# A hybrid decoder layer: expert gathers one block further ahead, other leads of the streams, adaLN loads by GpSimd, and a closing norm in groups of two

## The chip, the cores and the metric

The kernel runs on 1 core of one Trainium2 chip. The metric is the device time of one execution in microseconds (us), the median of several runs. Engines are named as in the profile: PE (TensorE matmul), PEld (TensorE weight load), DVE (VectorE), ACT (ScalarE), POOL (GpSimd) and SP (SyncE, which only issues transfers here).

## The reference

One decoder layer on 1024 tokens of width 1024, all in float32. `mod = silu(c) @ ada_w + ada_b` gives six rows of 1024 (shift, scale and gate for each half of the layer). The first half is a token mixer: FoX attention on 8 heads and an RWKV-7 recurrence on 8 heads, both from one input projection. The second half is a mixture of experts: 64 experts, 6 chosen per token, plus a shared one. The layer closes with an RMS norm.

```python
mod = jax.nn.silu(c) @ ada_w[l] + ada_b[l]
sh1, sc1, g1, sh2, sc2, g2 = jnp.split(mod[:, None, :], 6, axis=-1)
h = rms_norm(x, norm1_g[l]) * (1 + sc1) + sh1
z = h @ w_in[l]
...
x = x + g1 * (jnp.concatenate([y_fox, y_rwkv], axis=-1) @ w_out[l])
h = rms_norm(x, norm2_g[l]) * (1 + sc2) + sh2
x = x + g2 * moe_ffn(h, ...)    # sum over a token's experts of w_e * (silu(h Wg) * (h Wu)) Wd, plus the shared expert
return rms_norm(x, final_g)
```

## The kernel before, in words

**Order of the work.** Every engine executes its own queue in the order in which the program emits the instructions, and the kernel writes that order itself. `phase_a` holds some forty generators ("streams", one for each kind of work). `weave` (L1296) is a planner: it keeps a model clock for each engine, and always advances the stream whose next step is the earliest, after its lead has been taken off (L1361); a stream with a larger lead is emitted earlier than its place by the model clock. The leads are the numbers in the list at L1283 to L1292. They move instructions within each engine's queue, DMA issues among them; they add or remove none. `warm` (L169) puts dummy matmuls where the planner expects PE to be idle.

**Streams that the change touches.** `tok` (L756) turns RWKV features into token order by PE, copies them out by ACT and stores them. `main` (L670) forms these features, `gates` (L560) their gate, `merge` (L802) joins the halves of a triangular inverse, and `a4["gate"]` (L1484) gates the mixers' outputs ahead of the output projection. `adaln` (L1241) calls `mods_gen` (L1371): four rows of `mod`, each from eight tiles of 128x1024 weights (`mw`, 512 KB, three buffers) that SP loads (L1380); even tiles are multiplied and summed by DVE, odd ones scaled by ACT (L1393) and added by DVE. This runs beside the RWKV chain of 16 steps (`chain`, L918) and the attention.

**The expert blocks.** `experts` (L2091) runs 92 blocks: 8 of the shared expert (in token order), then 84 of the routed ones in a fixed order, each up to 128 rows. A routed block needs its slots (`need_s`, L2050: POOL gathers the token numbers and weights, tile `sl`, 8 buffers), its rows (`need_x`, L2060: POOL gathers rows of `d_h2` into `xg`, 4 buffers), and at its end `result` (L2022): DVE writes `ye` (3 buffers) and POOL adds it to `d_acc` in memory by an indirect DMA with `compute_op=add`. Every such addition goes to the same tensor, so it waits for the one before it to have landed. `need_t` (L2056) only makes a view of `sl`; it issues nothing. In iteration b, PE computes the gate and up products of block b (`up`), turns block b-1's activation (`act_t`), turns the rows of block b+1 (`turn`, tile `tp`), and computes block b-1's down product (`down`, tile `yd`). When an expert is new, DVE and ACT split its raw weights (`gate`, `up`, `down`) into two halves (L1897, L1898, L1904, L1905), and SP fetches weights three experts ahead. For b > 7, POOL's queue in iteration b holds, in this order:

```python
need_x(b + 3)                                             # L2124: gather rows, 3 blocks ahead
need_s(b + 5)                                             # L2126: gather slots, 5 blocks ahead
result(zs, blocks[b - 1][2], weight_of(b - 1), tis[b - 1])  # L2156: add block b-1 to d_acc
```

`dispatch` (L2077) gathers the slots of blocks 8 to 12 ahead of the loop. `rest` (L2170) handles overflow blocks, none in this input's profile.

**The closing norm.** `final` (L2198) loads eight tiles of 128x1024 from `d_acc`, squares them by ACT, forms the inverse root of a group of four by POOL (`rstd_pow`, L142), multiplies by DVE and stores.

Of the kernel before, what the change touches and what calls it, by code (L numbers as in the profile page):

```python
# [8 lines left out]
F32 = mybir.dt.float32  # L9
# [11 lines left out]
D = 1024  # L21
# [16 lines left out]
class Kern:  # L38
# [296 lines left out]
    def phase_a(self, psum):  # L335
# [51 lines left out]
        def loader():  # L387
            for j in range(1, len(tiles)):
                yield [("wait", ("raw used", j - 1))]
                load(j)  # L390
                yield [("set", ("raw", j))]
# [884 lines left out]
        def swap_project():  # L1276
# [4 lines left out]
            yield [("set", ("block pools", 0))]  # L1281

        self.weave([(swap_rwkv(), 9), (swap_fox(), 9),  # L1283
                    (chain(), -1.2), (inverse(), 2), (merge(), 2), (zts(), -2.3), (prods(), 1.5), (feeds(), 10.3),
                    (mixes(), 15.2), (kappa(), 1.2), (pre(), 1), (main(), 1),
                    (tok(), 2.2), (setup(), 0), (gates(), -0.5), (loader(), 0), (weights(), 3.3),
                    (fgate(), 1.8), (fk(), 1.8), (fv(), 0.8), (fq(), -0.5), (proj(), 0.6),
                    (ld(), 1.9), (rowmax(), 0.1), (exps(), 0.3), (onorm(), 0), (ynorm(), 1.1), (adaln(), -2),
                    (swap_ff(), 2.2), (swap_chain(), 0), (a4["router"](), -0.5), (a4["routes"](), -0.5), (a4["post"](), -0.2),
                    (a4["weights"](), 2), (swap_fox_out(), 9.6), (swap_project(), 16.6),  # L1290
                    (b["shared"](), -2.7), (b["dispatch"](), -0.2), (b["experts"](), -3.5),
                    (a4["gate"](), 0.8), (a4["project"](), -0.3), (a4["loads"](), -1)])  # L1292
        b["rest"]()

    @staticmethod
# [75 lines left out]
    def mods_gen(self, wp, pp):  # L1371

        nc, A = self.nc, self.A
        for m in range(4):
# [2 lines left out]

            def load(k):
                w = wp.tile([128, D], F32, name="mw", bufs=3)
                nc.sync.dma_start(w, A["ada_w"][0, k * 128:(k + 1) * 128, c0:c0 + D])  # L1380
                return w
            ws = [load(0), load(1)]
            yield [("DMA", 3.0)]
# [459 lines left out]
    def phase_b(self, pg, close_a4, h2):  # L1843
# [84 lines left out]
            yield [("set", ("shared w", 0))]  # L1928

        def slots(idx, n):  # L1930
            sl = B["fp"].tile([128, 2], F32, name="sl", bufs=8)
            nc.gpsimd.indirect_dma_start(out=sl[0:n], out_offset=None, in_=self.d_slot, in_offset=ind(idx[0:n]))  # L1932
            return sl

# [142 lines left out]
        def dispatch():  # L2077
            yield [("wait", ("route", 7))]
            expert_pools()
            yield from self.ranks(pg)  # L2080
            for k in range(1, 4):
                need_w(k)
            yield from self.leftover(pg)
            yield [("wait", ("block pools", 0))]
            for b in range(8, 13):
                need_s(b)
                yield [("POOL", 1.0)]
            yield [("DMA", 4.0)]
            yield [("set", ("slots", 0))]

        def experts():  # L2091
# [13 lines left out]
            for b in range(NB + 1):  # L2105
                if b < NB:
                    k, j, n = blocks[b]
                    m = max(n, MIN_M)
                    two = xt[1] is None
                    for s in up(xt, sets[k % 2], m):  # L2110
                        if b < 8:
                            yield s
                    z = B["z"]
                    if b < 5:
                        yield [("wait", ("T", blocks[b + 3][1]))]
                        need_x(b + 3)
                    elif b == 6:
                        yield [("wait", ("slots", 0))]
                        for i in range(8, 12):
                            need_t(i)  # L2120
                        need_x(8)
                        need_x(9)
                    elif b > 6:
                        need_x(b + 3)  # L2124
                    if b > 7:
                        need_s(b + 5)  # L2126
                    turnover = k + 1 < NK + 1 and (blocks[b - 1][0] != k if k else b == 6)
                    if turnover and k + 1 < NK:
                        work.append(split_gu(raws[k + 1], k + 1))
                    pieces(3)  # L2130
                    if turnover and b < 8:
                        yield [("~ACT", 1.7), ("~DVE*", 1.8)]
# [26 lines left out]
                if b < NB:  # L2159
                    if k and blocks[b - 1][0] != k:  # L2160
                        work.append(split_d(rawd[k]))
                        pieces(99)
                    if b > 7:
                        need_t(b + 4)
                    if turnover:
                        need_w(k + 4)
                    if turnover and b < 8:
                        yield [("~ACT", 2.0), ("~DVE", 2.3), ("~POOL", 1.0)]
# [29 lines left out]
    def final(self):  # L2198
        tc, nc, A = self.tc, self.nc, self.A
        with self.pool(name="fin", bufs=1) as fp:  # L2200
# [6 lines left out]
                nc.sync.dma_start(x, self.d_acc[i * 128:(i + 1) * 128, :])  # L2207
                xs.append(x)
            sm = fp.tile([128, 3, 8], F32, name="sm")
            for g in range(0, 8, 4):  # L2210
                gs = slice(g, g + 4)
                for i in range(g, g + 4):
                    sq = fp.tile([128, D], F32, name="sq", bufs=2)
                    nc.scalar.activation(sq, xs[i], AF.Square, accum_out=sm[:, 0, i:i + 1])  # L2214
                for _ in self.rstd_pow(sm[:, 1, gs], sm[:, 0, gs], D, 1e-6):
                    pass
                for i in range(g, g + 4):
                    nc.vector.scalar_tensor_tensor(xs[i], xs[i], sm[:, 1, i:i + 1], fg, op0=OP.mult, op1=OP.mult)  # L2218
                    nc.sync.dma_start(self.out[0, i * 128:(i + 1) * 128, :], xs[i])

# [41 lines left out]
```

## Time and profile before

| | us |
|---|---|
| median of 3 runs | 2097.12 |
| lowest and highest run | 2080.12, 2115.2 |
| the profiled execution, its own time | 2093.02 |
| its span, first to last instruction | 2091.1 |
| PE busy | 1858.6 (89%) |
| DVE busy | 1470.3 (70%) |
| ACT busy | 933.1 (45%) |
| POOL busy | 859.6 (41%) |
| mean granted TensorE clock, share of full | 0.918 |

The profiled execution took 1.9 us beyond its span, and was 4.1 us shorter than the median of the runs. Busy times are averages over stages with different limits. The stages on the span, about: start 0 to 50, projection and RWKV features to 450, chain and attention to 1000, output projection and routing to 1200, expert blocks to 2060, closing norm to 2091.

### The profile page before, as it was taken

The page shows a single profiled execution, that of the slowest core. Times are in us where ns is not written, and L with a number is a line of the kernel's source. Part 1 is how long each engine was busy: PE and PEld are TensorE (multiplying, and loading weights), DVE is VectorE, ACT ScalarE, POOL GpSimd, SP SyncE. Part 2 cuts the span into 40 slices and gives each one's busy share as a digit, 9 for nine tenths or more (in the row PEclk, how much of TensorE's full clock was granted, in tenths as well). Part 3 has the DMA queues.
Part 4 walks back from the last instruction along what each step waited for, and adds up shares of the span by engine and source line. Part 5 has one row for each costly group of instructions (what it writes and reads, how often), then busy time and mean ns, then how long its engine had stood idle before and what let it go on. Part 6 is the DMA issues. An engine that isn't in the chain of part 4 may idle for free. (4 is left out here: it accounts for less than half of the span.)

```text
span 2091.1 us, 28436 instructions
## 1 busy us (share of the span) xinstructions
PE 1858.6 (89%) x9729; PEld 1399.2 (67%) x9729; DVE 1470.3 (70%) x2561; ACT 933.1 (45%) x1431; POOL 859.6 (41%) x660
## 2 busy tenths in 40 slices
PE   3999999969997997997999799989988989989993
PEld 3777677747876664654787687767756767766771
DVE  7736867939457555656677758878767878878894
ACT  5443433312322332344323236556545656666673
POOL 1201110100012232335455634765656767766662
PEclk7999789969987888998999899999989999999997
DMA  7125345462756648964664589989889999988874
GB/s 270 36 81 126 88 111 129 131 156 71 216 148 183 190 123 237 133 195 137 229 211 147 159 277 322 314 256 318 293 261 309 304 305 307 326 297 297 307 242 174
DMA packets 268579, 440.03 MB, mean 210 GB/s; under 512 B 127445, under 2 KB 197161, under 8 KB 242450
## 3 DMA queue, kind: packets, MB, share of 16 engines
q1 hardware_dynamic: 210978, 365.47, 54.0%
q0 software_dynamic: 26176, 58.91, 12.4%
q10 hardware_dynamic: 31280, 13.83, 2.5%
q8 instruction: 78, 1.28, 0.3%
q14 instruction: 67, 0.55, 0.1%
HBM read 355.27 MB, written 94.90 MB: 215 GB/s over the span
## 5 line engine op out<-in xcount | busy, mean ns | idle before, releaser
L2028 POOL DMA_INDIRECT d_acc<-ye,sl x84 | 192.1, 2287 | 253.4 <-issue 56.2
L1932 POOL DMA_INDIRECT sl<-d_slot,d_sidx x84 | 201.6, 2400 | 27.5 <-issue 24.7
L1904 ACT ACTIVATE wdh<-down 128x1024 fp32r<-128x1024 f32 x128 | 128.7, 1053 | 82.2 <-PE yd L1976 82.2
L1898 DVE TENSOR_TENSOR gul<-up,guh 128x1024 fp32r<-128x1024 f32 x128 | 155.5, 1215 | 10.4 <-ACT guh L1897 9.7
L1940 POOL DMA_INDIRECT xg<-d_h,sl x84 | 149.0, 1774 | 25.6 <-issue 20.7
L1898 DVE TENSOR_TENSOR gul<-gate,guh 128x1024 fp32r<-128x1024 f32 x128 | 155.2, 1213 | 1.7 <-ACT guh L1897 1.7
L1905 DVE TENSOR_TENSOR wdl<-down,wdh 128x1024 fp32r<-128x1024 f32 x128 | 150.1, 1210 | 0.8
L2026 DVE SCALAR_TENSOR_TENSOR ye<-yd,sl,g 128x512 f32<-128x512 f32 (+12 forms) x168 | 120.2, 740 | 32.0 <-PE yd L1976 32.0
L1897 ACT ACTIVATE guh<-gate 128x1024 fp32r<-128x1024 f32 x128 | 134.1, 1047 | 18.8 <-DMA gate<-in_exp_w_gate_dram 18.8
L1976 PE MATMUL yd<-wdh,ah 128*128 128x512 f32 (+6 forms) x368 | 130.5, 438 | 8.5 <-ACT ah L2012 6.7
L1897 ACT ACTIVATE guh<-up 128x1024 fp32r<-128x1024 f32 x128 | 135.1, 1055 | 1.5 <-DMA up<-in_exp_w_up_dram 1.5
L450 PE MATMUL zp<-hTh,whi 128*128 128x512 f32 x480 | 132.4, 414 | 1.4 <-ACT whi L373 1.4
L450 PE MATMUL zp<-hTl,whi 128*128 128x512 f32 x480 | 132.1, 412 | 0.0
L450 PE MATMUL zp<-hTh,wlo 128*128 128x512 f32 x480 | 131.9, 413 | 0.0
L1976 PE MATMUL gu<-guh,xh 128*128 128x512 f32 (+6 forms) x504 | 127.3, 394 | 0.8 <-ACT xh L1959 0.5
L1976 PE MATMUL gu<-guh,xl 128*128 128x512 f32 (+6 forms) x504 | 127.4, 395 | 0.1
L1976 PE MATMUL yd<-wdh,al 128*128 128x512 f32 (+6 forms) x368 | 123.4, 418 | 4.2 <-DVE al L2014 3.7
L1976 PE MATMUL gu<-gul,xh 128*128 128x512 f32 (+6 forms) x504 | 127.0, 394 | 0.0
L1976 PE MATMUL yd<-wdl,ah 128*128 128x512 f32 (+6 forms) x368 | 122.3, 415 | 0.3 <-DVE wdl L1905 0.3
L2012 ACT ACTIVATE ah<-g 128x256 fp32r<-128x256 f32 (+5 forms) x92 | 31.2, 339 | 179.0 <-PE g L2010 178.3
L450 PEld LDWEIGHTS zp<-hTh,whi 128*128 128x128 f32 x480 | 92.6, 198 | 26.4 <-issue 5.5
L1976 PEld LDWEIGHTS gu<-guh,xh 128*128 128x128 f32 (+6 forms) x504 | 89.1, 177 | 29.1 <-ACT xh L1959 1.0
(477 smaller groups left out, 4238.9 us busy)
## 6 DMA issues: line engine op xcount, KB each, us to landing
gate<-in_exp_w_gate_dram SPq DMA_DIRECT2D x64, 1024.0 KB
up<-in_exp_w_up_dram SPq DMA_DIRECT2D x64, 1024.0 KB
down<-in_exp_w_down_dram SPq DMA_DIRECT2D x64, 1024.0 KB
mw<-in_ada_w_dram SPq DMA_DIRECT2D x32, 512.0 KB
wraw<-in_w_in_dram SPq DMA_DIRECT2D x30, 512.0 KB
xw<-in_ada_w_dram SPq DMA_DIRECT2D x8, 1024.0 KB
xw<-in_x_dram SPq DMA_DIRECT2D x8, 512.0 KB
fb<-d_fb SPq DMA_DIRECT2D x16, 256.0 KB
```

Of the source, the lines that this page charges most:

```text
L450: nc.tensor.matmul(z, a[:, d, :], b[:, d, hs], start=(n == 0 and d == 0), stop=(n == 2 and d == 7))
L1897: nc.scalar.activation(gh[:, qs, n, :], t[:, qs], AF.Copy)
L1898: nc.vector.tensor_sub(gl[:, qs, n, :], t[:, qs], gh[:, qs, n, :].bitcast(F32))
L1904: nc.scalar.activation(dh[:, j], raw[0][:, j], AF.Copy)
L1905: nc.vector.tensor_sub(dl[:, j], raw[0][:, j], dh[:, j].bitcast(F32))
L1932: nc.gpsimd.indirect_dma_start(out=sl[0:n], out_offset=None, in_=self.d_slot, in_offset=ind(idx[0:n]))
L1940: nc.gpsimd.indirect_dma_start(out=x[0:n], out_offset=None, in_=self.d_h2, in_offset=ind(ti), bounds_check=T - 1, oob_is_err=False)
L1976: nc.tensor.matmul(z, x[:, d, :], w[:, d, cs], start=(m == 0), stop=(m == 3 * n - 1))
L2012: nc.scalar.activation(ah[:, :, 0:n], tp[:, :, 0:n], AF.Copy)
L2026: nc.vector.scalar_tensor_tensor(y[0:n, hs], zs[h][0:n], wt, B["g2"][0:n, hs], op0=OP.mult, op1=OP.mult)
L2028: nc.gpsimd.indirect_dma_start(out=self.d_acc, out_offset=ind(ti), in_=y[0:n], in_offset=None, bounds_check=T - 1, oob_is_err=False, compu ...
```

## The change

It does five things.

1. Rows of a block are gathered four blocks ahead (`need_x(b + 4)`), slots six ahead (`need_s(b + 6)`), with nine `sl` buffers for eight; `dispatch` gathers six blocks' slots ahead of the loop. POOL's order within an iteration stays: rows, slots, addition.
2. Five leads: `merge` 2 to 2.1, `main` 1 to 0.9, `tok` 2.2 to 1.4, `gates` -0.5 to -0.6, `a4["gate"]` 0.8 to 0.9.
3. The 32 loads of `mw` are issued by POOL, not SP.
4. `need_t` is called beside `need_s`; it issues nothing.
5. The closing norm works in groups of two tiles.

```diff
-                    (chain(), -1.2), (inverse(), 2), (merge(), 2), (zts(), -2.3), (prods(), 1.5), (feeds(), 10.3),
-                    (mixes(), 15.2), (kappa(), 1.2), (pre(), 1), (main(), 1),
-                    (tok(), 2.2), (setup(), 0), (gates(), -0.5), (loader(), 0), (weights(), 3.3),
+                    (chain(), -1.2), (inverse(), 2), (merge(), 2.1), (zts(), -2.3), (prods(), 1.5), (feeds(), 10.3),
+                    (mixes(), 15.2), (kappa(), 1.2), (pre(), 1), (main(), 0.9),
+                    (tok(), 1.4), (setup(), 0), (gates(), -0.6), (loader(), 0), (weights(), 3.3),
...
-                    (a4["gate"](), 0.8), (a4["project"](), -0.3), (a4["loads"](), -1)])
+                    (a4["gate"](), 0.9), (a4["project"](), -0.3), (a4["loads"](), -1)])
...
-                nc.sync.dma_start(w, A["ada_w"][0, k * 128:(k + 1) * 128, c0:c0 + D])
+                nc.gpsimd.dma_start(w, A["ada_w"][0, k * 128:(k + 1) * 128, c0:c0 + D])
...
-            sl = B["fp"].tile([128, 2], F32, name="sl", bufs=8)
+            sl = B["fp"].tile([128, 2], F32, name="sl", bufs=9)
...
-            for b in range(8, 13):
+            for b in range(8, 14):
                 need_s(b)
...
                     elif b == 6:
                         yield [("wait", ("slots", 0))]
-                        for i in range(8, 12):
+                        for i in range(8, 14):
                             need_t(i)
-                        need_x(8)
-                        need_x(9)
+                        for i in range(8, 10):
+                            need_x(i)
                     elif b > 6:
-                        need_x(b + 3)
+                        if b == 7:
+                            need_x(10)
+                        need_x(b + 4)
                     if b > 7:
-                        need_s(b + 5)
+                        need_s(b + 6)
+                        need_t(b + 6)
...
-                    if b > 7:
-                        need_t(b + 4)
...
-            for g in range(0, 8, 4):
-                gs = slice(g, g + 4)
-                for i in range(g, g + 4):
+            for g in range(0, 8, 2):
+                gs = slice(g, g + 2)
+                for i in range(g, g + 2):
...
-                for i in range(g, g + 4):
+                for i in range(g, g + 2):
                     nc.vector.scalar_tensor_tensor(xs[i], xs[i], sm[:, 1, i:i + 1], fg, op0=OP.mult, op1=OP.mult)
```

## Rows read from the trace of the kernel before

**Rows 1.** Windows: busy us (count) of PE PEld DVE ACT POOL, PEclk, DMA share, GB/s
```profile
400.00:1200.00 800.00, 708.16 (x4206) 525.25 (x4205) 499.75 (x1124) 243.01 (x415) 263.35 (x327) 0.90 0.62 168
1240.00:2040.00 800.00, 747.56 (x3463) 567.70 (x3462) 652.14 (x841) 487.81 (x712) 517.33 (x235) 0.96 0.90 294
```
**Rows 2.** Waits of PE, 1195 to 2060: total us, times, longest us
```profile
PE tp L1965 <- DMA xg<-d_h,sl: 39.1, 11, 9.8
PE tp L1952 <- DMA xg<-d_h,sl: 6.4, 2, 5.7
```
**Rows 3.** Timeline of PE around one stall, then the window behind it
```profile
1531.45 1.68 PE L1965 MATMUL tp<-idf,xg 108*128 108x108 f32 x8 [9.84 <-DMA xg<-d_h,sl]
...
1536.41 1.05 PE L1976 MATMUL yd<-wdh,ah 128*128 128x512 f32 x2
...
1546.62 0.62 PE L1976 MATMUL yd<-wdh,ah 128*72 128x512 f32 x2
...
1530.00:1540.00 10.00, 8.55 (x28) 6.46 (x29) 3.48 (x6) 4.28 (x6) 5.59 (x5) 0.59 0.47 88
```
**Rows 4.** Timeline of POOL, 1657 to 1698: start, us, what, [idle before]
```profile
1657.42 1.44 POOL L2028 DMA_INDIRECT d_acc<-ye,sl  x1 [0.30 <-issue]
1659.17 0.96 POOL L1940 DMA_INDIRECT xg<-d_h,sl  x1 [0.31 <-issue]
1660.43 6.32 POOL L1932 DMA_INDIRECT sl<-d_slot,d_sidx  x1 [0.30 <-issue]
1667.06 1.50 POOL L2028 DMA_INDIRECT d_acc<-ye,sl  x1 [0.30 <-DVE xl L1968]
...
1678.67 1.50 POOL L2028 DMA_INDIRECT d_acc<-ye,sl  x1 [2.00 <-DVE gul L1898]
...
1697.86 7.28 POOL L2028 DMA_INDIRECT d_acc<-ye,sl  x1 [4.45 <-DVE ye L2026]
```
**Rows 5.** Timeline of DVE: `ye` of the additions at 1678.67 and 1697.86
```profile
1668.76 1.40 DVE L2026 SCALAR_TENSOR_TENSOR ye<-yd,sl,g 96x512 f32<-96x512 f32 x2
...
1686.47 0.75 DVE L2026 SCALAR_TENSOR_TENSOR ye<-yd,sl,g 128x512 f32<-128x512 f32 x1 [0.65 <-PE yd L1976]
```
**Rows 6.** Instructions on `d_acc` and their landing, then POOL's sequencer at L2028
```profile
L2028 POOL DMA_INDIRECT d_acc<-ye,sl x84: 1362/1608/7284, 1236.7 to 2059.3; - x84
DMA to landing us min/median/max: 4.0/8.8/17.8
...
L2028 POOLq EVENT_SEMAPHORE  x83: 17/5240/17366, 1237.6 to 2058.5; - x83
```
**Rows 7.** adaLN loads: SP issues, waits of ACT and PE, one stall, POOL's own loads
```profile
L1380 SPq DMA_DIRECT2D mw<-in_ada_w_dram x32: 327/449/1693, 545.1 to 808.8; - x32
...
ACT mw L1393 <- DMA mw<-in_ada_w_dram: 40.2, 9, 10.5
...
PE pm L174 <- ACT yt L964: 11.1, 1, 11.1
...
786.20 2.17 SPq L1380 DMA_DIRECT2D mw<-in_ada_w_dram  x2
...
792.29 1.15 ACT L1393 ACTIVATE mw<-mw,sc 128x1024 f32<-128x1024 f32 x1 [10.48 <-DMA mw<-in_ada_w_dram]
...
L992 POOL DMA_DIRECT2D d_y<-yt x8: 597/620/670, 604.8 to 915.2; - x8
```
**Rows 8.** Waits of PE, 450 to 700: the longest stall of the feature streams
```profile
PE g L616 <- ACT sqk L1038: 15.3, 4, 13.5
```
**Rows 9.** The closing norm: end of the second square, POOL, DVE, memory rate
```profile
2071.98 0.19 ACT L2214 ACTIVATION_READ_ACCUMULATOR sq<-x 128x1 f32 x1
...
2075.16 1.04 POOL L146 TENSOR_TENSOR sm<-sm,blk 128x4 f32<-128x4 f32 x1
...
2076.24 4.87 DVE L2218 SCALAR_TENSOR_TENSOR x<-x,sm,fg 128x1024 f32<-128x1024 f32 x4 [17.31 <-POOL sm L146]
...
2070.00:2076.00 6.00, 0.00 (x0) 0.00 (x0) 0.00 (x0) 4.52 (x8) 1.03 (x2) 0.50 1.03 419
```

## The prediction

> **What bounds the kernel now.** I read the page's 40 slices first, then windows by stage, then who PE waits for in each stage, and at last the timelines of POOL, DVE and PE side by side. The reader is to see two stages that matter. From 400 to 1200 PE is busy 708.16 of 800 us, at a clock of 0.90; part of that is dummy matmuls, so a long wait there is a real loss, but no single engine is the bound. From 1240 to 2040, the expert blocks, PE is busy 747.56 of 800 us, DVE 652.14, POOL 517.33, and the DMA engines 0.90 of the time [rows 1]. By the busy shares this is a PE-bound stage, with one visible defect: PE waits for gathered rows 13 times, 39.1 + 6.4 = 45.5 us [rows 2].
>
> The timeline of POOL says something else. The 84 additions into `d_acc` start between 1236.7 and 2059.3, so one every (2059.3 - 1236.7) / 83 = 9.91 us, and one takes 8.8 us (median) from issue to landing [rows 6]. The next may not start before. POOL's sequencer waits 5.24 us (median) at this instruction, up to 17.4 [rows 6]. It seldom waits for data: the `ye` of the addition at 1678.67 was written by 1668.76 + 1.40 = 1670.16, 8.5 us before; that of the one at 1697.86 by 1686.47 + 0.75 = 1687.22, 10.6 us before [rows 4, 5]. Where the landing doesn't hold an addition, POOL itself does: a slots gather that met a full DVE took 6.32 us, and the addition followed 0.30 us later [rows 4]. So the additions form a chain of their own, which runs without a pause and mostly behind its data. PE's need per block is smaller: 747.56 us over the 800 / 9.91 = 81 blocks of that window is 9.2 us [rows 1, 6], and that holds matmuls at the low clock. I read the stage as bound by this chain on POOL and the DMA engines, at 9.9 us per block, and PE's waits for rows as the way in which PE is held to that pace: POOL issues a gather behind an addition, so when the additions are late, the rows are late.
>
> **The change, part by part.** All sums are against the profiled execution, 2093.02 us, which is 4.1 below the median of the runs; I carry the differences over to the median.
>
> *Gathers one block further ahead.* POOL executes the same three instructions per block in the same order. Rows for a given block come one cycle sooner, about 9.9 us. The longest wait is 9.8 [rows 2], so at first every wait for rows should go. What is late next? PE would then run at about 9.2 us per block against 9.9, and draw ahead by 0.7 us a block. The limit is `ye`: three buffers, so DVE may write a block's `ye` only when the addition of three blocks before has landed. That stops DVE when the additions are more than 3 x 9.2 - 8.8 = 19 us behind their data; they are 8.5 and 10.6 in the two cases above. From there DVE waits at L2026, `yd` stays full, and PE waits at its down product instead. The chain has no step that becomes shorter. Its end moves only by what lies at its edges: near the end PE, DVE and the weight transfers would be done up to one block earlier, and the last few additions land in a quieter memory, nearer to the 4.0 us minimum than to 8.8 [rows 6]. The bounds are 0, and all the waits with the clock behind them. For the clock: after the 9.84 us wait the window stands at 0.59, between the two levels 0.5 (1.2 GHz) and 1 (2.4 GHz), and a pair of `yd` matmuls takes 1.05 us where it takes 0.62 later [rows 3]. Six pairs to a block make 6 x 0.43 = 2.6 us per wait, 34 us for 13 at the most; the shorter waits will cost less, so I estimate 20. The upper bound is thus 45.5 + 20 = 65 us. I take 3, because the row it is nearest to is the wait of 5.24 us at every addition, which the change leaves in place. One more slots gather stands ahead of the first rows: it costs from 0 to the 6.3 us of the slow one [rows 4]; before the loop DVE has gaps, so I count it within the 3.
>
> *adaLN loads by POOL.* SP now issues 32 loads, 0.45 us (median) each, among its other transfers [rows 7]. ACT waits for them nine times, 40.2 us; only one such wait reaches PE visibly: ACT waits 10.48 us until 792.29, and PE 11.1 us [rows 7]. Of the loads of that moment, two were issued at 786.20 in 2.17 us, though ACT had been free since 792.29 - 10.48 = 781.8. Without SP's queue ahead they could go 4 to 6 us sooner; I take 5 us saved on PE (bounds: 0, and 11.1 plus 2.6 for the clock). On POOL a direct load should cost what its stores of half the size do, 0.62 us (0.60 to 0.67, all eight alike) [rows 7], or twice that: 20 to 43 us over the 264 us from 545.1 to 808.8 [rows 7]. POOL is busy only 263.35 of 800 us in this stage [rows 1], and this hides it. If POOL is held up there, see the second rival. SP's queue loses 32 issues, which starts its later transfers a little sooner; I count nothing for that, as the engines behind it mostly wait for each other.
>
> *Five leads.* They permute instructions in the queues from about 50 to 1000 us; nothing is added. No row prices a permutation. The nearest is the longest single wait of these streams: PE 13.5 us for ACT's square of a FoX key tile [rows 8]. One such wait can go or come, so the bounds are -13.5 and +13.5. I take 0: `tok` is the one lead that moves much, and what it feeds (the bonus term, the token-order copies) isn't what PE waits for in that row.
>
> *Closing norm.* The first multiplications start when two squares are done (2071.98 + 0.19 = 2072.17), not four; L146 then starts some 0.3 us later and DVE 1.1 us after that, at 2073.5 for 2076.24: 2.7 us sooner [rows 9]. After the last square, two multiplications are left for four: half of 4.87, another 2.4 [rows 9]. But the loads still run at that time at 419 GB/s with the DMA engines full (1.03) [rows 9]; stores begun there push the loads back by as much. The bounds are 0 and 2.7 + 2.4 = 5; I take 2.
>
> The 9th `sl` buffer keeps the old distance between a slot's gather and its last use, and `need_t` issues nothing: 0.
>
> The sum is -3 - 5 + 0 - 2 = -10 us: 2083 for an execution like the profiled one, 2087 for the median.
>
> **The rivals.** *First: the waits for rows are worth their full price.* PE is the bound, as its busy share of 0.93 says, and the additions speed up once PE does. For it: PE's waits name `xg` and nothing else of size [rows 2]. Against it: additions 8 to 10 us behind data that lay ready [rows 4, 5]. It gives 65 us in place of 3: 2097 - 65 - 7 = 2025; where only half comes, 2057.
>
> *Second, on the other side: POOL's queue delays the adaLN loads.* POOL takes instructions in order, and in this stage its queue holds normalisations and the chain's scaling, which wait for DVE. A load that stands behind one of these is late, ACT stops at L1393 in front of the chain's copies, and PE stops as at 794. One such stop costs 11.1 us [rows 7]. It decides from the fourth stop on: 4 x 11.1 = 44 us, so 2097 - 5 + 44 = 2136; five give 2147. For it: nine waits of ACT exist already, of which a few more microseconds would carry several through to PE. Against it: POOL's load, and the even 0.60 to 0.67 us of its own stores there. The Trainium skill speaks against this move (DMA: Bandwidth & Descriptors, section "SWDGE vs HWDGE vs iDMA"): a transfer issued by GpSimd has its descriptors written by software into SBUF, and VectorE can lock GpSimd out of that; one issued by SP is immune. The trace agrees in the expert stage (6.32 us for one gather) and not around the loads (no store above 0.67). By the rule the cost would be up to 32 x 6.32 = 202 us of POOL's time, and this rival would be the forecast.
>
> *Third: the leads decide.* One or two waits of 13.5 us come or go with nothing else changed: 2087 - 27 = 2060 to 2087 + 27 = 2114.
>
> **How the numbers follow.** Forecast 0.64 (its own range 2070 to 2108), first rival 0.18, third 0.10, second 0.08. The range leaves out the better half of the first rival and the second: 2045 to 2120. A measurement of this kernel tells about 2%, or 42 us, from no change: faster than 2055 is nearly all of the first rival, 0.17; slower than 2139 is the worse part of the second, 0.05; the rest, 0.78, lies within.
>
> **What would show it.** In the profile after, PE's waits on `xg` should be gone or a fraction of 45.5 us, while additions still start every 9.7 to 10 us and their sequencer's median wait stays at 5 us or grows; new waits should stand at `ye` or `yd`. If the additions come every 9.3 us or less, the first rival is right and my reading of the chain wrong. ACT's waits at L1393 should fall below 40 us and PE's 11.1 us wait shrink; if PE shows several waits behind L1393, the second rival holds. DVE should start the closing multiplications some 2.7 us sooner after the loads begin. A difference of more than 14 us ahead of 1000 us that no wait at L1393 explains would be the leads.

## The result and the profile after

The changed kernel takes 2112.97 us (median of 20 runs, 2100.79 to 2132.69), the kernel before 2095.01 (20 runs in the same sittings, 2077.02 to 2115.20). The ratio is 1.0084, 95% interval 1.0059 to 1.0109: some 18 us slower, where I had forecast 10 faster. It lies within my range, but the time moved the other way. A ratio compares undisturbed executions alone; as executions of one kernel scatter by 1 to 2 per cent here and those over 1.5% above its fastest are left out, the medians, which I give beside it, can lie further apart than the ratio says.

The profiled execution of the changed kernel has a span of 2101.2 us, 10 more than before. First the windows of the expert blocks (columns as in [rows 1]), then PE's waits in 1195 to 2070 (total us, times, longest), which answer to [rows 2]:

```profile
1240.00:2040.00 800.00, 743.43 (x3420) 559.54 (x3418) 642.81 (x832) 483.82 (x707) 520.05 (x229) 0.96 0.90 292
```

```profile
PE tp L1965 <- DMA xg<-d_h,sl: 34.2, 12, 6.3
PE yd L1976 <- DVE al L2014: 16.6, 24, 2.9
...
PE tp L1952 <- DMA xg<-d_h,sl: 1.9, 2, 1.6
```

PE's waits for rows fell from 45.5 us to 36.1 only, and PE's busy time in the window fell by 4 us instead of rising. A wait that was 3.7 us in the kernel before (PE at `yd` for `al`) is now 16.6. In the kernel before:

```profile
PE yd L1976 <- DVE al L2014: 3.7, 12, 0.4
```

The waits of DVE in 1240 to 2070, first in the changed kernel, then all that it had at `ye` in the kernel before, say why:

```profile
DVE ye L2026 <- DMA d_acc<-ye,sl: 37.1, 16, 7.7
DVE ye L2026 <- issue: 36.3, 9, 8.1
DVE ye L2026 <- PE yd L1976: 26.2, 24, 2.8
```

```profile
DVE ye L2026 <- PE yd L1976: 31.3, 46, 2.0
```

In the kernel before only the last of these stood there (31.3 us). DVE now stops at `ye` for the landing of additions, 37.1 us by name; the 36.3 without a releaser did not stand there before either. By the timelines an addition now starts 17.7 us (median) behind the end of its `ye`, where it was 7.1. The additions, as in [rows 6]:

```profile
L2028 POOLq EVENT_SEMAPHORE  x83: 17/4983/15758, 1241.4 to 2064.4; - x83
...
L2028 POOL DMA_INDIRECT d_acc<-ye,sl x84: 1322/1618/7827, 1235.4 to 2069.1; - x84
```

They start 1.3 us sooner and end 9.8 later: (2069.1 - 1235.4) / 83 = 10.04 us each against 9.91. So the loss of this execution lies in the expert loop, and in the chain of additions. The sequencer's median wait there is 4.98 us, against 5.24; and the time from issue to landing, of those additions for which the trace has it, is 8.7 us (median) against 8.8, so the further gathers don't make the additions land later behind their issue. One place shows what happens in it. DVE, then POOL, about 1535 (start, us, what, idle before):

```profile
1532.66 1.22 DVE L1898 TENSOR_TENSOR gul<-up,guh 128x1024 fp32r<-128x1024 f32 x1
1534.26 1.40 DVE L2026 SCALAR_TENSOR_TENSOR ye<-yd,sl,g 56x512 f32<-56x512 f32 x2 [0.38 <-DMA d_acc<-ye,sl]
1535.59 2.34 DVE L1905 TENSOR_TENSOR wdl<-down,wdh 128x1024 fp32r<-128x1024 f32 x2
1537.86 1.21 DVE L1898 TENSOR_TENSOR gul<-gate,guh 128x1024 fp32r<-128x1024 f32 x1
1538.99 1.21 DVE L1898 TENSOR_TENSOR gul<-up,guh 128x1024 fp32r<-128x1024 f32 x1
1540.13 1.21 DVE L1898 TENSOR_TENSOR gul<-gate,guh 128x1024 fp32r<-128x1024 f32 x1
```

```profile
1535.00 7.82 POOL L2028 DMA_INDIRECT d_acc<-ye,sl  x1 [2.74 <-DVE ye L2026]
```

The reader is to see one event with two followers. The landing of an addition lets DVE write `ye` (1534.26) and lets POOL issue the next addition (1535.00). Behind `ye` DVE has the five weight subtractions of a new expert, both inputs in SBUF, 1.2 us each. The first starts at 1535.59, while POOL is still issuing, and POOL is held beyond the end of the burst (1540.13 + 1.21 = 1541.34): 7.82 us for an instruction whose median is 1.62. In the kernel before such bursts met additions too (7.28 us at the most, [rows 4]), but at any distance. Behind a stop the distance is nearly always the same. But the same distance doesn't always cost. An earlier place of the same trace, DVE, then POOL:

```profile
1420.66 1.41 DVE L2026 SCALAR_TENSOR_TENSOR ye<-yd,sl,g 128x512 f32<-128x512 f32 x2 [1.80 <-DMA d_acc<-ye,sl]
1421.99 2.35 DVE L1905 TENSOR_TENSOR wdl<-down,wdh 128x1024 fp32r<-128x1024 f32 x2
```

```profile
1421.39 1.64 POOL L2028 DMA_INDIRECT d_acc<-ye,sl  x1 [5.33 <-issue]
```

Here the same five subtractions start 0.60 us behind the start of the addition, and it takes 1.64 us. In the changed kernel 14 additions have such a burst of five 0.5 to 0.8 us behind their start; five of them took over 7 us, the other nine 1.4 to 2.0. What decides between the two isn't shown.

The adaLN loads, ACT's wait for them in 540 to 860 and PE's waits in 700 to 900, against [rows 7]:

```profile
L1380 POOL DMA_DIRECT2D mw<-in_ada_w_dram x32: 527/547/683, 546.4 to 804.6; - x32
```

```profile
ACT mw L1393 <- DMA mw<-in_ada_w_dram: 16.7, 5, 6.4
```

```profile
PE s L1214 <- ACT os L1209: 10.0, 4, 5.7
PE pm L174 <- ACT yt L964: 7.4, 1, 7.4
```

The first of these two in the kernel before:

```profile
PE s L1214 <- ACT os L1209: 3.3, 4, 1.7
```

ACT's waits fell from 40.2 us to 16.7 and PE's single wait from 11.1 to 7.4, while another of PE's waits for ACT, at L1214, rose from 3.3 to 10.0: the one fell by 3.7 us, the other rose by 6.7.

The closing norm, SP's loads and stores, then DVE, against [rows 9]:

```profile
2073.58 5.99 SPq L2208 DMA_DIRECT2D x<-d_acc  x8
2084.23 11.02 SPq L2220 DMA_DIRECT2D out_dram<-x  x8
```

```profile
2082.92 2.48 DVE L2219 SCALAR_TENSOR_TENSOR x<-x,sm,fg 128x1024 f32<-128x1024 f32 x2 [17.20 <-POOL sm L146]
...
2092.41 2.48 DVE L2219 SCALAR_TENSOR_TENSOR x<-x,sm,fg 128x1024 f32<-128x1024 f32 x2 [0.59 <-POOL sm L146]
```

DVE starts 9.34 us after the first load is issued, where it was 2076.24 - 2064.00 = 12.24; but from that load to the end it is 2101.2 - 2073.58 = 27.6 us, against 27.1.

### The profile page after: what moved, and what is told of

It is laid out like the page before. It is cut to its first block, busy times and chain, and to the rows that moved or that the text cites. A ratio compares the mean times of both kernels' runs of the same rounds, so it can differ in the third digit from the quotient of the medians.

```text
span 2101.2 us, 28428 instructions
## 1 busy us (share of the span) xinstructions
PE 1853.3 (88%) x9716; PEld 1388.9 (66%) x9716; DVE 1466.3 (70%) x2561; ACT 934.2 (44%) x1431; POOL 890.7 (42%) x696
## 5 line engine op out<-in xcount | busy, mean ns | idle before, releaser
L2028 POOL DMA_INDIRECT d_acc<-ye,sl x84 | 204.7, 2437 | 259.4 <-issue 67.7
L1940 POOL DMA_INDIRECT xg<-d_h,sl x84 | 186.3, 2218 | 25.8 <-issue 21.0
L2026 DVE SCALAR_TENSOR_TENSOR ye<-yd,sl,g 128x512 f32<-128x512 f32 (+12 forms) x168 | 119.0, 740 | 100.4 <-DMA d_acc<-ye,sl 37.1
L1932 POOL DMA_INDIRECT sl<-d_slot,d_sidx x84 | 159.3, 1896 | 27.5 <-issue 24.4
L1976 PE MATMUL yd<-wdh,al 128*128 128x512 f32 (+6 forms) x368 | 125.6, 424 | 17.2 <-DVE al L2014 16.6
L2012 ACT ACTIVATE ah<-g 128x256 fp32r<-128x256 f32 (+5 forms) x92 | 31.3, 340 | 184.5 <-PE g L2010 183.8
```

The costliest lines, as they stand in the source:

```text
L1940: nc.gpsimd.indirect_dma_start(out=x[0:n], out_offset=None, in_=self.d_h2, in_offset=ind(ti), bounds_check=T - 1, oob_is_err=False)
L1976: nc.tensor.matmul(z, x[:, d, :], w[:, d, cs], start=(m == 0), stop=(m == 3 * n - 1))
L2012: nc.scalar.activation(ah[:, :, 0:n], tp[:, :, 0:n], AF.Copy)
L2026: nc.vector.scalar_tensor_tensor(y[0:n, hs], zs[h][0:n], wt, B["g2"][0:n, hs], op0=OP.mult, op1=OP.mult)
L2028: nc.gpsimd.indirect_dma_start(out=self.d_acc, out_offset=ind(ti), in_=y[0:n], in_offset=None, bounds_check=T - 1, oob_is_err=False, compu ...
```

## The experiments

**The change taken apart.** Two theories for the 18 us: A, the further gathers disturb the chain of additions; B, the leads or the loads. The first four kernels each add one part of the change to the kernel before.

Gathers alone:

```diff
+need_x(b + 4); need_s(b + 6); need_t(b + 6)
-need_x(b + 3); need_s(b + 5); need_t(b + 4)
...
```

> Only the gathers one block further ahead (with the ninth sl buffer and the earlier need_t), all else as before. Theory A (the chain of additions bounds the expert stage, and drawing ahead only makes DVE stop at ye and disturb POOL): the whole loss of the change lies here, 10 to 20 us slower than before, ratio 1.005 to 1.010; 84 additions at 10.0 us or more each; DVE waits at ye for additions, PE's waits on xg below 40 us. Theory B (the loss comes from the leads or the loads, and the gathers are neutral as forecast): within 5 us of before, additions at 9.9 us.

Measured: 2114.29 us against 2091.25, ratio 1.0112 (1.0053 to 1.0170). This rests on six executions, of which two (2090.22 and 2095.66) lie near the median of the kernel before and one (3111.62) far from all others. The profiled one was the shortest (2090.22 us, additions every 9.90 us). DVE's waits at `ye` for additions are there (23.6 us by name), with five additions of over 7.5 us, and PE's waits for rows are 28.5; yet this execution is no longer than the kernel before.

Leads alone:

```diff
-(merge(), 2), (main(), 1), (tok(), 2.2), (gates(), -0.5), (a4["gate"](), 0.8)
+(merge(), 2.1), (main(), 0.9), (tok(), 1.4), (gates(), -0.6), (a4["gate"](), 0.9)
```

> Only the five leads. Theory A: no difference, within 5 us of before. Theory B: 10 to 18 us slower, with the first addition of the expert stage later by that much than 1236.7 us, since the streams end before it.

Measured: 2098.60, ratio 1.0038 (1.0011 to 1.0066), so 2 to 14 us slower: between the two theories. PE's wait of [rows 8] is 14.8 us there, 13.5 before, and the first addition starts at 1239.9, 3.2 us later.

Loads by GpSimd alone:

```diff
-nc.sync.dma_start(w, A["ada_w"]...)
+nc.gpsimd.dma_start(w, A["ada_w"]...)
```

> Only the adaLN weight loads issued by GpSimd. Theory A: 0 to 5 us faster, as forecast, PE's 11.1 us wait at 794 us shorter. Theory B: slower by up to 11 us, one more stop of ACT carried to PE.

Measured: 2085.39, ratio 0.9964 (0.9935 to 0.9993): 7.5 us faster by the ratio. PE's wait of 11.1 us is 7.3 in its profile, ACT's 40.2 are 11.2; but PE's wait at L1214 is 9.3 for 3.3 here too, and the first addition starts at 1234.7, only 2.0 us sooner. So most of the 7.5 us isn't found in this profile.

Closing norm alone:

```diff
-for g in range(0, 8, 4):
+for g in range(0, 8, 2):
...
```

> Only the closing norm in groups of two. Forecast: 2 us faster (0 to 5). The profiled execution of the changed kernel speaks for nothing gained: from the first load to the end 27.6 us against 27.1, since the two further rounds of pow stand in DVE's way. So within 1 us of before, ratio 0.9995 to 1.0005.

Measured: 2093.17, ratio 1.0023 (0.9990 to 1.0057): no difference that this tells.

Two more kernels take a part away from the whole change. Without its gathers:

```diff
-need_x(b + 4); need_s(b + 6); need_t(b + 6)
+need_x(b + 3); need_s(b + 5); need_t(b + 4)
...
```

> The whole change without its gathers: the five leads, the loads by GpSimd and the closing norm in twos. From the parts measured alone (ratios 1.0038, 0.9964, 1.0023): product 1.0025, 0 to 10 us slower than before. If the gathers carry the loss only together with the other parts, this would be faster than before.

Measured: 2105.81 (four runs, 2075.37 to 2108.31) against 2092.94. Four runs so far apart decide nothing.

Without its leads:

```diff
-(tok(), 1.4)
+(tok(), 2.2)
...
```

> The whole change without the five leads: gathers ahead, loads by GpSimd, closing norm in twos. If the gathers carry the loss: ratio 1.005 to 1.012, as for the gathers alone. If the leads carry half or more of it: 1.000 to 1.004. From the parts alone: 1.0112 x 0.9964 x 1.0023 = 1.010.

Measured: 2116.70 against 2099.84 by the medians, ratio 1.0025 (0.9981 to 1.0069). The medians speak for the gathers, the interval holds the other answer as well. Of the parts, then, the gathers alone show a loss of 11 to 36 us, the leads of 2 to 14, the loads a gain of 1 to 14. The product of the four ratios is 1.0137, above the 1.0084 measured but within these widths. The other way round, 1.0084 / (1.0038 x 0.9964 x 1.0023) = 1.0059 leaves some 12 us for the gathers, with a width of about the same size. So the gathers carry most of the loss as far as can be told; the leads can have a share.

**Is the chain of additions the bound?** Two accumulators: an addition then waits for the one before the last. The eight blocks of the shared expert are stored plainly into the second one, which makes its start.

```diff
+acc = self.d_acc2 if b > 0 and b % 2 else self.d_acc
-nc.gpsimd.indirect_dma_start(out=self.d_acc, ..., compute_op=OP.add)
+nc.gpsimd.indirect_dma_start(out=acc, ..., compute_op=OP.add)
...
+nc.vector.tensor_add(x, x, x2)
```

> The kernel before with two accumulators: the shared blocks' results are written to a second DRAM tensor, the expert blocks add to the first and the second by turns, and the closing norm adds the two. An addition then waits for the landing of the one before the last only. Chain theory (each addition starts 0.8 us after the landing of the one before, and this sets the stage): the additions come every 9.3 us or less (PE's need per block is 9.2), 84 x 0.6 = 50 us saved or more, less some 10 us for 8 more loads at the end: 2040 to 2055 us. Rival (the memory traffic of the additions and gathers itself is the bound, and the order among additions costs nothing): they still come every 9.7 us or more, and the time is 5 to 15 us above before.

Measured: 2049.51 us, ratio 0.9786 (0.9757 to 0.9816): 45 us faster, as the chain theory said. Its additions, then PE's waits for rows:

```profile
L2034 POOLq EVENT_SEMAPHORE  x84: 17/17/43, 1234.3 to 2005.4; - x84
...
L2034 POOL DMA_INDIRECT d_acc<-ye,sl x84: 1347/1659/6877, 1241.9 to 2012.5; - x84
```

```profile
PE tp L1966 <- DMA xg<-d_h,sl: 3.0, 5, 1.3
...
PE tp L1953 <- DMA xg<-d_h,sl: 1.1, 2, 0.9
```

The window of [rows 1] in this kernel:

```profile
1240.00:2040.00 800.00, 755.00 (x3579) 571.79 (x3577) 675.10 (x876) 503.51 (x742) 588.17 (x242) 0.98 0.92 307
```

The sequencer's wait fell from 5.24 us [rows 6] to 0.02, the spacing to (2012.5 - 1241.9) / 83 = 9.28 us. And PE's waits for rows fell from 45.5 us to 4.1, though no gather was moved. They were the chain's doing.

The same with the gathers one block further ahead (the two edits above together):

```diff
+need_x(b + 4); need_s(b + 6); need_t(b + 6)
...
+acc = self.d_acc2 if b > 0 and b % 2 else self.d_acc
...
```

> The same two accumulators, with the gathers one block further ahead. Chain theory: with the chain gone, PE's waits for rows have a price, and the kernel is 20 to 45 us faster than with two accumulators alone; DVE's waits at ye are gone. Rival (the further gathers disturb the stage by themselves, chain or not): 5 to 25 us slower than with two accumulators alone.

Measured: 2044.25, ratio 0.9762 (0.9735 to 0.9789). It is the fastest of all kernels here, but not the 20 to 45 us below the one before it: the intervals overlap. There was no wait for rows left to remove. The rival is out too: with the chain gone the further gathers cost nothing. With the loads by GpSimd as well:

```diff
+nc.gpsimd.dma_start(w, A["ada_w"]...)
```

> Two accumulators, gathers one block further ahead, and the adaLN loads by GpSimd; no leads, no closing norm in twos. If the parts add up (0.9762 x 0.9964): 2033 to 2042 us. If the loads gain nothing once the stage behind them is another: 2044 as without them.

Measured: 2054.91 against 2099.84, ratio 0.9779 (0.9731 to 0.9827): the loads add nothing that shows.

**Does the stop at ye cost?** Two `ye` buffers in the kernel before, no gather moved:

```diff
-name="ye", bufs=3
+name="ye", bufs=2
```

> The kernel before with two ye buffers in place of three: DVE then has to stop at ye in the kernel before as well, since additions stand 7.1 us (median) and up to 18.7 us behind their data there. If the stop of DVE at ye is what costs the changed kernel its 18 us: 15 us or more slower, with DVE waits at ye of 40 us or more. If a stop at ye is without price as long as the chain of additions runs on: within 5 us of before.

Measured: 2105.04 against 2092.94, ratio 1.0026 (0.9990 to 1.0062): below the 15 us, not told from nothing. Its profile is worth more than its time. DVE's waits at `ye` in 1240 to 2070, and DVE and POOL at one of the stops:

```profile
DVE ye L2026 <- DMA d_acc<-ye,sl: 50.3, 15, 6.7
...
DVE ye L2026 <- issue: 35.8, 11, 7.6
```

```profile
1559.98 1.41 DVE L2026 SCALAR_TENSOR_TENSOR ye<-yd,sl,g 108x512 f32<-108x512 f32 x2 [2.06 <-issue]
1561.31 2.35 DVE L1905 TENSOR_TENSOR wdl<-down,wdh 128x1024 fp32r<-128x1024 f32 x2
```

```profile
1560.73 7.70 POOL L2028 DMA_INDIRECT d_acc<-ye,sl  x1 [3.33 <-DVE ye L2026]
```

`ye` 0.75 us ahead of the addition, `wdl` 0.58 behind its start: the phase of the changed kernel (0.74 and 0.59 at 1535.00), in a kernel that shares nothing with it but the stop. I went through the additions of all kernels with one accumulator and this order of the instructions, one profile each. The columns: from the start of the 1st addition to that of the 25th, on to the 61st, and to the 84th and last, in us; the issue times of the 25th to the 60th added up; and how many of the 84 took 7.5 us or more to issue.

| kernel | 1st to 25th | to 61st | to 84th | issue, 25th to 60th | 7.5 us or more |
|---|---|---|---|---|---|
| before | 249.7 | 369.7 | 203.2 | 84.8 | 0 |
| leads alone | 241.4 | 373.1 | 203.2 | 97.3 | 0 |
| loads alone | 252.6 | 368.8 | 207.9 | 82.2 | 0 |
| norm alone | 246.5 | 368.0 | 206.2 | 76.6 | 0 |
| change without gathers | 247.9 | 383.0 | 197.3 | 89.7 | 0 |
| subtractions in another form (below) | 254.2 | 359.3 | 202.9 | 73.9 | 0 |
| changed kernel | 250.3 | 388.5 | 194.9 | 105.5 | 5 |
| gathers alone | 244.4 | 382.7 | 194.3 | 98.0 | 5 |
| change without leads | 252.0 | 390.0 | 200.2 | 109.9 | 7 |
| two `ye` buffers | 241.1 | 385.2 | 205.0 | 102.4 | 6 |

The four kernels in which DVE stops at `ye` need 386.6 us on average for the middle stretch, the six others 370.3: 16 more. Their issue times there add up to 104.0 against 84.1: 20 more, enough to account for it. The last stretch is 7 us shorter in the three kernels with the gathers ahead (196.5 against 203.5), and not in the one with two `ye` buffers. So in these profiles the gathers ahead lose some 16 us in the middle and gain 7 at the end of the loop.

This is weaker than it looks. The groups touch: the change without its gathers, with no stop at `ye` and no such issue, needs 383.0 us for the middle stretch, and the gathers alone 382.7; the leads alone have 97.3 us of issue times there, the gathers alone 98.0. The mark of 7.5 us flatters the split as well: from 7.0 us on the counts are 6, 5, 9 and 8 with the stop and 4, 2, 5, 3, 0 and 2 without, and from 3 us on 15 to 20 against 12 to 17. And over the whole window 1240 to 2040 POOL's indirect DMAs take as long in the changed kernel as before, 520.0 us: those of additions 191.0 for 183.7, of rows 179.0 for 142.8, of slots 150.0 for 193.5. The bursts catch other instructions of POOL, not more of them. In the four kernels with the stop, 51 additions have a burst of five 0.5 to 0.8 us behind their start, and 23 of them were held for over 7.5 us; in the six without it there are three, none of them held.

**What holds POOL?** The subtractions in another form:

```diff
-nc.vector.tensor_sub(gl, t, gh)
+nc.vector.scalar_tensor_tensor(gl, t, 1.0, gh, op0=OP.mult, op1=OP.subtract)
```

> The kernel before with the same subtractions written as scalar_tensor_tensor (times 1, minus). If this form leaves GpSimd its way into SBUF: no indirect DMA above 3 us, additions every 9.3 us or less, 40 us faster or more. If two inputs in SBUF hold it whatever the operation: the same counts (some 43 of 240 above 3 us) and a time within 5 us of before.

Measured: 2096.98 against 2099.84, ratio 0.9993 (0.9964 to 1.0022); 41 of its 308 indirect DMAs took over 3 us, 43 of 308 in the kernel before (the 240 of the expectation counts too few). The form makes no difference.

The subtractions spread over the block (`pieces(1)` between `al`, the two `xl` and `act`):

```diff
-pieces(3)
+pieces(3 if b < 8 else 1)
...
```

> The kernel before with the weight splits of the expert loop spread: in place of up to five of the 1.21 us subtractions with both inputs in SBUF back to back (two wdl, three gul), at most two, the others between al, xl and act. Theory (GpSimd cannot issue its indirect DMAs during such a burst; that is what makes 43 of 240 take 3 to 7 us and lengthens the chain of additions): the additions' mean issue falls from 2.29 us towards 1.7, their median stays at 1.6, they come every 9.5 us or less, and the kernel is 20 to 50 us faster. Rival (the bursts only coincide; the chain is set by the landing): the spacing stays at 9.8 to 10 and the time within 5 us, or is worse where PE waits for the later splits.

Measured: 2110.57 against 2099.84, ratio 1.0024 (0.9982 to 1.0065): no gain of 20 us. In its profile 24 of 308 indirect DMAs took over 3 us, but the additions' mean issue is 2.27 us as before (2.29). The spread order shifts ACT's copies as well, so this is no clean test of the hold.

The traces gave a theory P, phase lock: one landing releases DVE at `ye` and POOL's next addition, and DVE's burst then catches that addition. If it makes up the loss, taking the burst away from behind `ye` gives the loss back. Another order on DVE, `wdl` ahead of `ye` and the first three `gul` behind `xl`, with the gathers ahead:

```diff
-pieces(3)
+pieces(3 if b < 8 else 0)
 xt = turn(...)
+pieces(3 if b > 7 else 0)
...
+work.append(split_d(rawd[k])); pieces(99)
 result(...)
```

> Gathers one block further ahead, and another order on DVE in the expert loop: the two wdl subtractions ahead of the two writes of ye in place of behind them, and the first three gul behind xl in place of ahead of al. After a stop at ye come then ye, al and xl, which read PSUM, and the next subtraction from SBUF starts 2 us or more after the addition. Theory P: no addition of 7.6 to 7.9 us behind a stop of DVE at ye, the additions' mean issue 2.0 us or less (2.4 to 2.7 without), spacing 9.8 us or less, and the time 15 us or more below the gathers alone: at or below the kernel before, ratio 0.990 to 1.001. Rival (the gathers themselves lengthen the landings): the issue falls but the time stays 10 to 20 us above before.

Measured: 2106.22 against 2094.43, ratio 1.0054 (1.0025 to 1.0083). The mean issue fell to 2.1 us, near the 2.0 said, but the additions came every 9.96 us, not 9.8, and the time stayed above before. The same order in the kernel before:

```diff
 result(...)
-work.append(split_d(rawd[k])); pieces(99)
...
```

> The same order on DVE in the kernel before, where DVE does not stop at ye. Theory P: less to gain, as the bursts meet the additions in any phase there; the issue falls from 2.29 to 2.0 us, 0 to 15 us faster, and less is gained than with the gathers ahead. Rival: the order is worth the same in both kernels, or costs in both (PE waits for the later gul).

Measured: 2118.77, ratio 1.0114 (1.0067 to 1.0161). The order costs 24 us by itself; PE's waits in 1240 to 2070 show where:

```profile
PE gu L1976 <- ACT guh L1897: 30.4, 35, 1.0
PE tp L1965 <- DMA xg<-d_h,sl: 19.8, 4, 10.1
PE yd L1976 <- DVE ye L2026: 13.6, 17, 1.4
```

It moved ACT's `guh` copies behind the turn, and PE waits for them. My expectation for the pair had left that out. Long issues aren't the stop's alone, either: four additions took over 7.5 us in this kernel (up to 8.90), in which DVE never stops at `ye` for an addition. Against each other the two kernels are worth something: with this order the further gathers gain 12.6 us by the medians (the intervals just overlap), and PE's waits for rows fall from 25.7 us to 8.1, as the change had meant them to. With two accumulators the order is dearer still:

```diff
+pieces(3 if b > 7 else 0)
+acc = self.d_acc2 if b > 0 and b % 2 else self.d_acc
...
```

> Two accumulators, gathers ahead, and that order on DVE. With two accumulators an addition does not wait for the one before, and PE is busy 0.94 of the stage; so little is left: 2035 to 2050 us, ratio 0.970 to 0.980 (0.9762 without). If the order makes PE wait for gul, it shows here first: above 2055.

Measured: 2110.03, ratio 1.0059 (1.0027 to 1.0091), 66 us above the same without the order: the "shows here first" case. And only the `gul` moved, with the gathers ahead:

```diff
-pieces(3)
+pieces(3 if b < 8 else 0)
...
```

> Gathers ahead, only the first three gul moved behind xl; the two wdl stay right behind ye. Theory P: the lock stays, additions of 4.3 to 5 us behind each stop of DVE at ye (two subtractions long, no longer five), so about half of the loss is left: 5 to 15 us above before. Rival (it is the count of subtractions in a row, not their phase): as good as with both moved.

Measured: 2112.37, ratio 1.0073 (1.0044 to 1.0101), within the 5 to 15 us of the first theory; as the order has a price of its own, that is no proof.

Last, all orders as they were and three PSUM memsets between `ye` and `wdl` where an expert begins, with the gathers ahead and without:

```diff
 work.append(split_d(rawd[k]))
+for _ in range(3 if b > 7 else 0):
+    nc.vector.memset(B["g"], 0.0)
```

> Gathers one block further ahead, and a gap of three PSUM memsets (some 0.45 us each by the memsets of 912 ns for 1024 columns) between ye and wdl. Theory P: after a stop of DVE at ye the first wdl then starts 2 us after the addition in place of 0.6, the addition of 1.4 to 1.6 us is through, none behind a stop takes 7.6 to 7.9, and the time falls 10 to 25 us below the gathers alone, to a ratio of 0.998 to 1.006, though DVE has 60 us more to do. Rival (the stop itself, or the gathers, cost, not the phase): 1.008 to 1.020, as the gathers alone or worse by the added work.

> The same gap in the kernel before, without the gathers ahead. Theory P: the phase of bursts and additions is loose there, so the gap helps some additions and hurts others: within 10 us of before, and the gathers ahead with the gap cost 3 us or less against this. Rival: the gathers ahead cost 15 us or more against this, gap or not.

Measured: 2145.41 and 2151.11 against 2091.84, ratios 1.0286 (1.0238 to 1.0335) and 1.0279 (1.0230 to 1.0328). Groups of POOL in 1240 to 2100 with the gathers ahead, its additions, and DVE's memsets:

```profile
L2029 POOL DMA_INDIRECT d_acc<-ye,sl x81 | 136.8, 1689 | 429.3 <-DVE ye L2027 404.8 <-DVE g L2167 15.1 <-DVE gul L1898 6.6
L1940 POOL DMA_INDIRECT xg<-d_h,sl x77 | 128.0, 1663 | 23.7 <-issue 21.6 <-PE gu L1984 1.2 <-PE tp L1965 0.6
```

```profile
L2029 POOL DMA_INDIRECT d_acc<-ye,sl x84: 1321/1528/2690, 1236.0 to 2110.0; - x84
```

```profile
L2167 DVE MEMSET g<- 128x512 f32 x174 | 84.4, 485 | 27.2 <-DVE g L2167 21.1
```

The long issues are gone: no addition above 2.69 us. But the memsets take DVE 84.4 + 27.2 = 112 us with the idle time before them, not 60, as an expert begins 58 times; POOL now waits for `ye` (404.8 us of its idle time) and PE for DVE's `al` (77.9 us), so I read DVE as the bound. The gathers ahead cost nothing in this pair, and the absolute time missed both theories.

## Why the prediction was wrong

**The bound: right.** The additions form the chain that sets the expert stage, and PE's waits for rows follow from it: two accumulators took 45 us off and nearly all of those waits with them. Their spacing without the chain, 9.28 us, is near my 9.2 for PE's need per block, but that is in part luck: by the sum that gave 9.2, PE's need there is 755.00 us over 800 / 9.28 = 86 blocks, 8.8 us. What sets the pace with two accumulators isn't shown.

**The first rival: out.** With the gathers ahead the waits for rows did not go (36.1 of 45.5 us), because, as I read it, POOL issues a gather behind an addition and the additions came later. With two accumulators, where they did go, moving the gathers as well changed the median by 5 us, within the intervals.

**The gathers: the step that failed.** What would be late next I had right: DVE stops at `ye` (additions 17.7 us behind their data, near the limit of 19 that I worked out), and PE waits at the down product, if only because DVE is late with `al`. Wrong was what followed: "The chain has no step that becomes shorter. Its end moves only by what lies at its edges", with 0 as the lower bound and 3 us as the gain. I asked whether a step becomes shorter and not whether one becomes longer; that the chain could grow I put at nothing without a reason. The runs showed a chain that grew: 10.04 us per addition for 9.91 in the changed kernel, and a loss of 11 to 36 us with the gathers alone.

Which step grew is shown in part. The stop at `ye` ties DVE's burst to the start of an addition, and some of these then take 7.6 to 7.9 us to issue; in the profiles that goes with 16 us more in the middle of the loop, and the edge that I priced at 3 gave 7. I had the row in hand: 6.32 us for a gather that met a full DVE [rows 4], and used it for POOL's pace only. The Trainium skill has a mechanism for it (SBUF — State Buffer, section "Who interferes with whom"): a DVE instruction with two SBUF inputs contends with a GpSimd instruction that reads SBUF, since its second input comes through the read interface that the two share. The 7.82 us under `wdl` and `gul` agree with it; that 28 of the 51 additions with the same burst at the same distance were not held, it doesn't explain by itself.

What is shown and what isn't: the fixed distance stands in every profile with the stop, and the further gathers cost nothing in the three settings where DVE hardly stops or the chain is not the bound (two accumulators, the other order, the gap). That the long issues make up the loss is argued, not shown. No run took the distance alone away and gave the 18 us back, since both attempts brought a new bound; two `ye` buffers, with the same long issues and the same middle stretch, are not measurably slower as a whole; and the shortest execution of the gathers alone has the long issues without the loss. So the cause of the loss inside the chain remains open.

**The loads: right by the number, less so by the wait.** 5 us forecast, 7.5 measured (1 to 14). With the loads alone PE's wait shrank by 3.8 us of its 11.1, as I had said, but its wait at L1214 grew by 6.0, so the waits by name don't show where the gain comes from; and on top of two accumulators the loads gained nothing. POOL's issues took 0.55 us (median), at most 0.68 in the changed kernel, near the lower of the two prices that I allowed; the second rival is out.

**The leads: 0 with bounds of 13.5.** Measured +8 us (2 to 14), within the bounds; the third rival's place, the wait at the FoX key square, moved from 13.5 to 14.8 us only. That the changed kernel came out near the third rival's 2114 us is chance. What the 8 us are is open.

**The closing norm: 2 us forecast, none found.** The multiplications start 2.9 us sooner, as worked out (2.7), but the end does not follow. DVE now waits between the groups for POOL's L146 (0.59 us ahead of the last one), and the stores take 11.02 us to issue in place of 9.97.

The sum was off by 28 us. The sign hangs on the gathers as far as the parts can tell; the leads, which I could not price, took away what the loads gave.

## What to carry to other kernels

When waits for a transfer stand on a busy engine, ask whether a serial chain behind them sets their pace; if so, break the chain (a second accumulator, 45 us here) instead of issuing earlier. Where an earlier issue shifts the stall to the next buffer, ask what else the event that ends this stall releases: two engines started by one landing stood at a nearly fixed distance from then on, and if they get in each other's way there, it can happen again and again. It did so in 23 of 51 places here, and its price in the whole was not isolated. A chain that can't become shorter can still become longer: a lower bound of 0 needs a reason too.

## What was not expected of the hardware

The same burst at the same distance behind the start of an addition held it to 7.8 us in one place and left it at 1.6 in another, in one trace (1535.00 and 1421.39). Writing the subtraction as scalar_tensor_tensor held GpSimd just as tensor_sub did (longest addition 7.23 us against 7.28). Three memsets of PSUM, 0.49 us each, between `ye` and the burst took away all long issues, with DVE busier than before: with the gathers ahead, POOL's busy time in 1240 to 2040 fell from 529.28 us to 365.08. And two additions in flight at a time moved more through the same DMA engines than one: 307 GB/s at a busy share of 0.92, against 294 at 0.90 [rows 1].
